# Latent attention of one transformer block: scores of four heads side by side, value products in pairs, output projection k by k

## The chip, the cores and the metric

The kernel runs on one core of a Trainium2 chip. The metric is the device time of one execution in microseconds (us). Five engines work beside each other, each through its own instructions in a fixed order: PE (TensorE, matmuls), DVE (VectorE), ACT (ScalarE), POOL (GpSimd) and SP, whose queue issues the loads of the weights. An instruction that waits for another engine holds back all that stand behind it on its own engine.

## The reference, cut to what matters

256 tokens of width 1024 go through a mixer, a feed-forward layer, latent attention, a second feed-forward layer, and then a second block with attention and a gated feed-forward layer. The change touches latent attention alone:

```
cq, ckv, kr = split(h @ w_in, [384, 640])
q  = (rms_norm(cq, q_g) @ w_uq).reshape(b, s, 16, 64 + 32)
kv = (rms_norm(ckv, kv_g) @ w_ukv).reshape(b, s, 16, 64 + 64)
q_rope, k_rope = apply_rope(q[..., 64:]), apply_rope(kr)
qf = concat([q[..., :64], q_rope]);  kf = concat([kv[..., :64], k_rope for every head])
pr = softmax(qf @ kf * 96 ** -0.5)
x  = x + (pr @ kv[..., 64:]) @ w_out
```

So each of the 16 heads has 64 plain and 32 rotated rows for its scores; the rotated key is the same for all heads.

## The kernel before

All activations are kept with features on the 128 partitions and the 256 tokens along the row. A weight comes as a chunk of up to 1 MB from HBM (`raw`), and is split on the core into a high part (`whi`, ACT, L149) and the rest (`wlo`, DVE or POOL, L152). Each product is then three matmuls in a one-pass type (`three`, L367 to L370: high by high, high by low, low by high). Three `raw` buffers and four pairs of split buffers go round; the SP queue issues the next load when the split before it is done (`Stream`, L125).

The program is built by a scheduler that sets the order on each engine from its own timeline. `Later` (L79) holds pieces of work until so many "ticks" of matmul time have been emitted.

Latent attention stands between the two feed-forward layers:

- `tgemm(XH, XL, KB, 5, c_evac, ...)` (L975): the input projection, five tiles of 128 features (two for keys and values, three for queries). `c_evac` (L944) scales each tile by its gain, splits it into `ch` and `cl`, squares it and lets POOL add the squares. For the two key tiles the split waits until the statistic is known (`kv_split`, L938).
- `rkv_chain` and `rq_chain`: a column sum by PE (L917), a few small operations on DVE, a power on POOL (L925), and for the keys a broadcast over partitions by PE (L342) from `dg`, which DVE makes (L335, L336).
- `thin` (L363) and `fold` (L980) give the rotated key of 32 rows, which a DMA copies to 16 heads (L989).
- `uq_evac` and `uk_evac` put the queries and keys head by head into `qT` and `kT`, 96 rows each.
- Then the heads, one at a time (`attend`, L1068): `sc` makes the scores by two matmuls of 96 rows in full fp32 (L1028; the trace has two records for each), DVE takes the maximum (L1032, L1033), ACT the exponential (L1035), DVE divides by the sum (L1041, L1043), `tr` transposes four blocks (L1050), DVE or ACT copies them (L1052), `pv` multiplies with the values (L1062), and for every second head ACT and DVE split the result (L1065, L1066). Stages of different heads are staggered.
- The output projection is a `tgemm` over eight tiles (L1095 ff.), with the last heads between its first matmuls, and `residual` (L490) adds each result to `x`.

The second block's attention (L1214 to L1290) already works on two heads at once: `sc(j)` sets 64 rows of one head beside 64 rows of the other (L1219) and `pv(j)` sets the 64 value columns of the two heads beside each other (L1269). PSUM holds eight tiles of 128x512: four of the tag `mm`, four of the tag `aux`.

Of the kernel before, what the change touches and what calls it, by code (L numbers as in the profile page):

```python
# [30 lines left out]
PAD_W = 4800 // 4  # L31
# [162 lines left out]
def block_kernel(ctx, tc, a, out):  # L194
# [40 lines left out]
    fold = gap.tile([P, 32], F32, name="fold")  # L235
    cosT = gap.tile([P, T], F32, name="cosT")
# [5 lines left out]
    for n in ("w_va", "w_qk01", "w_qk23", "w_vb", "w_u", "w_oa", "w_ab_out", "w1_0", "w2_0", "w_cin",  # L242
              "w_uq", "w_uk", "w_uv", "w_c_out", "w1_1", "w2_1", "w_qk2", "w_v2",
              "w_o2", "w_gu4", "w_gu", "w_down"):
# [37 lines left out]
    for i in range(2, 4):  # L282
        pool.tensor_tensor(fold, fold, ident[:, 32 * i:32 * i + 32], op=ALU.add)

# [610 lines left out]
    with tc.tile_pool(name="mla", bufs=1) as ap:  # L895
        mpc = tc.tile_pool(name="mlt", bufs=2)
        mp = mpc.__enter__()
        ckv = mp.tile([P, 2, T], F32, tag="ckv", name="ckv", bufs=1)
        ch = ap.tile([P, 5, T], F32R, name="ch")
        cl = ap.tile([P, 5, T], F32R, name="cl")  # L900
        qT = ap.tile([96, NH, T], F32, name="qT")
        kT = ap.tile([96, NH, T], F32, name="kT")
        v = ap.tile([P, 2, D], F32, name="v")
        yh = ap.tile([P, KB, T], F32R, name="yh")
        yl = ap.tile([P, KB, T], F32R, name="yl")
# [32 lines left out]
        def kv_split():  # L938
            for j in range(2):
                dve.tensor_tensor(ckv[:, j], ckv[:, j], rbc[1], op=ALU.mult)  # L940
                act.activation(ch[:, j], ckv[:, j], AF.Copy)
                dve.tensor_tensor(cl[:, j], ckv[:, j], ch[:, j].bitcast(F32), op=ALU.subtract)

        def c_evac(m, ps):  # L944
            for i in range(ps.shape[1]):
# [4 lines left out]
                if kv:  # L950
                    act.activation(ckv[:, j], ps[:, i], AF.Copy, scale=g)
                else:
                    act.activation(ch[:, j], ps[:, i], AF.Copy, scale=g)
                    dve.scalar_tensor_tensor(cl[:, j], ps[:, i], g, ch[:, j].bitcast(F32), op0=ALU.mult,
                                             op1=ALU.subtract)
# [8 lines left out]
                if j == 1:  # L964
                    later(2.0, rkv_chain)
                if j == 4:
                    later(3.5, rq_chain)
# [7 lines left out]
        tgemm(XH, XL, KB, 5, c_evac, lead=4, psums={4: auxt})  # L975

        kr4 = tmp.tile([P, T], F32, tag="rs", name="kr4")
        act.activation(kr4, thin(wkr, "c_norm"), AF.Copy)
        pk = auxt()
        pe.matmul(pk[0:32, 0:T], fold, kr4, start=True, stop=True)  # L980
        SHUF = [(i + 16) % 32 for i in range(32)]
        kr = mp.tile([32, T], F32, tag="kr", name="kr", bufs=1)
        dve.tensor_tensor(kr, pk[0:32, 0:T], rbc[0][0:32], op=ALU.mult)
        k2 = mp.tile([32, T], F32, tag="k2", name="k2", bufs=1)
        dve.stream_shuffle(k2, kr, SHUF)
        pool.tensor_tensor(kr, kr, cosT[0:32], op=ALU.mult)
        dve.tensor_tensor(k2, k2, sinT[0:32], op=ALU.mult)
        dve.tensor_tensor(kr, kr, k2, op=ALU.add)
        nc.sync.dma_start(kT[64:96], spread(kr.unsqueeze(1), 1, NH))  # L989

        def uq_evac(m, ps):

            if m < 4:
                for i in range(2):
                    qs = mp.tile([P, T], F32, tag="qs", name="qs")
                    q2 = mp.tile([P, T], F32, tag="q2", name="q2")
                    act.activation(qs, ps[:, i], AF.Copy)
                    dve.stream_shuffle(q2, qs, SHUF)
                    pool.tensor_tensor(qs, qs, cosT, op=ALU.mult)
                    dve.tensor_tensor(q2, q2, sinT, op=ALU.mult)  # L1000
                    for j in range(4):
                        rr = slice(32 * j, 32 * j + 32)
                        (dve if j < 2 else pool).tensor_tensor(qT[64:96, 4 * (m + i) + j], qs[rr], q2[rr], op=ALU.add)
            else:
                h = 2 * (m - 4)
                q4 = qT[0:64, h:h + 4].rearrange("p (a b) t -> p a b t", b=2)
                act.activation(q4[:, :, 0], ps[0:64], AF.Copy)
                act.activation(q4[:, :, 1], ps[64:128], AF.Copy)

        tgemm(per_k(ch, 5)[2:5], per_k(cl, 5)[2:5], 3, 12, uq_evac, bpc=12)  # L1010

        def uk_evac(m, ps):
            h = 2 * m
            k4 = kT[0:64, h:h + 4].rearrange("p (a b) t -> p a b t", b=2)
            act.activation(k4[:, :, 0], ps[0:64], AF.Copy)
            dve.tensor_copy(k4[:, :, 1], ps[64:128])

        tgemm(per_k(ch, 5)[0:2], per_k(cl, 5)[0:2], 2, 8, uk_evac)
# [4 lines left out]
        st_p, st_t = {}, {}  # L1023

        def sc(h):
            ps = mmt().rearrange("p (a b) -> p a b", a=2)
            for qt in range(2):
                pe.matmul(ps[:, qt], qT[:, h, qt * P:(qt + 1) * P], kT[:, h], start=True, stop=True)  # L1028
            mx = mp.tile([P, 2], F32, tag="mx", name="mx", bufs=3)
            sm = mp.tile([P, 2], F32, tag="sm", name="sm", bufs=4)  # L1030
            pr = mp.tile([P, 2, T], F32, tag="pr", name="pr", bufs=4)
            dve.tensor_reduce(mx, ps, axis=AX, op=ALU.max)  # L1032
            dve.tensor_tensor(mx, mx, nsrq, op=ALU.mult)  # L1033
            for qt in range(2):
                S.behind = act.activation(pr[:, qt], ps[:, qt], AF.Exp, scale=srq[:, qt:qt + 1],  # L1035
                                          bias=mx[:, qt:qt + 1], accum_out=sm[:, qt:qt + 1])
            st_p[h] = (pr, sm)

        def nrm(h):
            pr, sm = st_p[h]  # L1040
            dve.reciprocal(sm, sm)  # L1041
            for qt in range(2):
                dve.tensor_scalar(pr[:, qt], pr[:, qt], sm[:, qt:qt + 1], None, op0=ALU.mult)  # L1043

        def tr(h):
            pr, sm = st_p.pop(h)
            ps = auxt().rearrange("p (a b) -> p a b", a=2)
            for kt in range(2):
                for qt in range(2):
                    pe.transpose(ps[:, kt, qt * P:(qt + 1) * P], pr[:, qt, kt * P:(kt + 1) * P], ident)  # L1050
            pT = mp.tile([P, 2, T], F32, tag="pT", name="pT", bufs=2)
            (act.activation(pT, ps, AF.Copy) if h % 2 else dve.tensor_copy(pT, ps))  # L1052
            st_t[h] = pT

        def pv(h):
            pT = st_t.pop(h)
            if h % 2 == 0:
                state["o"] = auxt()
            o = state["o"]
            rr = slice(64 * (h % 2), 64 * (h % 2) + 64)  # L1060
            for kt in range(2):
                pe.matmul(o[rr, 0:T], v[:, kt, h * 64:(h + 1) * 64], pT[:, kt], start=kt == 0, stop=kt == 1)  # L1062
            if h % 2:
                j = h // 2
                act.activation(yh[:, j], o[:, 0:T], AF.Copy)  # L1065
                dve.tensor_tensor(yl[:, j], o[:, 0:T], yh[:, j].bitcast(F32), op=ALU.subtract)  # L1066

        def attend(i):  # L1068

            if 0 <= i - 3 < NH:  # L1070
                tr(i - 3)
            if 0 <= i - 4 < NH:
                pv(i - 4)
            if 0 <= i - 1 < NH:
                nrm(i - 1)
            if i < NH:
                sc(i)

        wh, wl = S.get()
        for n in range(2):  # L1080
            for tt in range(2):
                ts = slice(tt * P, (tt + 1) * P)
                ps = auxt()
                for k in range(2):
                    s = slice(k * D + n * 512, k * D + n * 512 + 512)
                    pe.matmul(ps, ch[:, k, ts], wh[:, s], start=k == 0, stop=False)
                    pe.matmul(ps, ch[:, k, ts], wl[:, s], start=False, stop=False)
                    pe.matmul(ps, cl[:, k, ts], wh[:, s], start=False, stop=k == 1)
                act.activation(v[:, tt, n * 512:(n + 1) * 512], ps, AF.Copy)
                if n + tt:  # L1090
                    attend(n + n * tt + (1 - n) * (tt - 1))
        S.done()
        for i in range(3, NH):
            attend(i)
# [425 lines left out]
```

## Time and profile before

| | us |
|---|---|
| three runs, median (lowest to highest) | 915.9 (913.51 to 918.45) |
| the profiled execution, its own time | 918.1 |
| span from first to last instruction in it | 916.4 |
| PE busy in the span | 889.9 (97%) |
| DVE, ACT, POOL busy | 583.3, 481.3, 268.0 |
| mean granted clock of TensorE, share of full | 0.988 |

Busy time of PE counts matmuls that overlap in the pipeline, so the distance from one start to the next is what a matmul costs. In a row of the timeline, the first number is the start in us from the span's start, the second how long the row's instructions lasted together, "x4" how many records it merges; at the end stands, in brackets, how long the engine was idle before and on what it waited.

### The profile page before, as it was taken

How to read it: one execution, taken by the hardware profiler on the slowest of the kernel's cores; microseconds unless marked ns; L12 is line 12 of the kernel's file. 1: busy time of each engine (PE TensorE's matmuls, PEld its weight loads, DVE VectorE, ACT ScalarE, POOL GpSimd, SP SyncE). 2: the span in 40 equal slices, each digit the busy share in tenths (PEclk: the TensorE clock that was granted, in tenths of full speed). 3: DMA queues.
4: the chain of work that ended last, by engine and by line, in shares of the span. 5: the costliest groups of instructions: out<-in, count | busy, mean ns of one | idle time of the engine just before them, and what ended most of it. 6: DMA issues, size and time to landing. Idle time of an engine off the chain costs nothing.

```text
span 916.4 us, 16411 instructions
## 1 busy us (share of the span) xinstructions
PE 889.9 (97%) x6680; PEld 824.1 (90%) x6680; DVE 583.3 (64%) x943; ACT 481.3 (53%) x848; POOL 268.0 (29%) x269
## 2 busy tenths in 40 slices
PE   7899999999999998999999999999999999999997
PEld 5788999999999987679999999999967789999885
DVE  7697889555555379846755555547783766666442
ACT  6675467555444275756555544424376665544331
POOL 5876733333011266047333301110147000000000
PEclk9999999999999998999999999999999999999999
DMA  8543454655554336014565555549432465555521
GB/s 293 199 150 126 142 187 161 230 189 191 188 191 164 109 116 230 1 57 150 207 211 189 191 187 191 185 164 248 189 138 93 174 246 191 194 185 189 189 82 46
DMA packets 26107, 154.90 MB, mean 169 GB/s; under 512 B 2752, under 2 KB 5744, under 8 KB 8752
## 3 DMA queue, kind: packets, MB, share of 16 engines
q1 hardware_dynamic: 22704, 148.70, 45.6%
q10 hardware_dynamic: 3040, 4.36, 1.9%
q8 instruction: 52, 0.85, 0.4%
q0 software_dynamic: 288, 0.79, 0.3%
q14 instruction: 23, 0.19, 0.1%
HBM read 152.25 MB, written 1.07 MB: 167 GB/s over the span
## 4 chain that ended last, share of the span: by engine, by line
PE 58%; DVE 1%; issue 0%; ACT 0%; DVEq 0%; POOLq 0%; ACTq 0%
PE mm L368 12%; PE mm L369 12%; PE mm L370 12%; PE aux L466 2%; PE aux L465 2%; PE aux L467 2%; PE mm L1028 2%; PE aux L1062 2%; PE mm L430 2%; PE mm L432 2%; PE mm L431 2%; PE aux L1050 1%; PE mm L465 1%; PE mm L467 1%; PE mm L466 1%; PE aux L1219 1%
## 5 line engine op out<-in xcount | busy, mean ns | idle before, releaser
L149 ACT ACTIVATE whi<-raw 128x1024 fp32r<-128x1024 f32 (+3 forms) x318 | 284.9, 949 | 240.2 <-PE mm L369 157.0
L152 DVE TENSOR_TENSOR wlo<-raw,whi 128x1024 fp32r<-128x1024 f32 (+2 forms) x254 | 307.5, 1246 | 124.4 <-ACT whi L149 122.7
L368 PE MATMUL mm<-xh,whi 128*128 128x256 f32 x1072 | 301.4, 281 | 0.8 <-DVE head L494 0.8
L369 PE MATMUL mm<-xl,whi 128*128 128x256 f32 x1072 | 299.1, 279 | 0.0
L370 PE MATMUL mm<-xh,wlo 128*128 128x256 f32 x1072 | 299.0, 279 | 0.0
L370 PEld LDWEIGHTS mm<-xh,wlo 128*128 128x128 f32 x1072 | 203.9, 190 | 0.0
L368 PEld LDWEIGHTS mm<-xh,whi 128*128 128x128 f32 x1072 | 202.0, 188 | 1.7 <-DVE head L494 1.0
L369 PEld LDWEIGHTS mm<-xl,whi 128*128 128x128 f32 x1072 | 202.0, 188 | 0.2
L368 PE MATMUL mm<-hh,whi 128*128 128x256 f32 x512 | 143.9, 281 | 0.0
L369 PE MATMUL mm<-hl,whi 128*128 128x256 f32 x512 | 143.9, 281 | 0.0
L370 PE MATMUL mm<-hh,wlo 128*128 128x256 f32 x512 | 143.9, 281 | 0.0
L152 POOL TENSOR_TENSOR wlo<-raw,whi 128x512 fp32r<-128x512 f32 (+2 forms) x64 | 84.5, 1349 | 67.0 <-ACT whi L149 66.9
L370 PEld LDWEIGHTS mm<-hh,wlo 128*128 128x128 f32 x512 | 98.3, 192 | 0.0
L368 PEld LDWEIGHTS mm<-hh,whi 128*128 128x128 f32 x512 | 96.1, 188 | 0.0
L369 PEld LDWEIGHTS mm<-hl,whi 128*128 128x128 f32 x512 | 96.1, 188 | 0.0
L519 POOL TENSOR_TENSOR fu<-ft 128x512 f32<-128x512 f32 (+1 forms) x36 | 54.7, 1521 | 119.3 <-ACT ft L517 111.6
L313 POOL TENSOR_TENSOR s_acc<-s_acc,sq 128x256 f32<-128x256 f32 x37 | 43.9, 1193 | 155.2 <-ACT sq L312 144.6
L1120 POOL TENSOR_TENSOR r<-v,nhalf 128x1 f32<-128x1 f32 x4 | 2.2, 557 | 193.5 <-DVE v L1119 193.5
L430 PE MATMUL mm<-whi,xh 128*128 128x512 f32 x96 | 39.1, 424 | 1.9 <-ACT whi L149 1.9
L431 PE MATMUL mm<-wlo,xh 128*128 128x512 f32 x96 | 38.1, 400 | 2.2 <-DVE wlo L152 2.2
L520 DVE TENSOR_TENSOR hl<-fu,hh 128x512 fp32r<-128x512 f32 (+1 forms) x36 | 24.1, 675 | 23.4 <-POOL fu L519 23.4
L432 PE MATMUL mm<-whi,xl 128*128 128x512 f32 x96 | 37.9, 398 | 0.6 <-DVE xl L1329 0.6
(370 smaller groups left out, 1355.7 us busy)
## 6 DMA issues: line engine op xcount, KB each, us to landing
raw<-in_w_dram SPq DMA_DIRECT2D x64, 1024.0 KB, 4.8
raw<-in_w_gu_dram SPq DMA_DIRECT2D x22, 1024.0 KB, 4.8
raw<-in_w_qk_dram SPq DMA_DIRECT2D x12, 1024.0 KB, 6.1
raw<-in_w_down_dram SPq DMA_DIRECT2D x11, 1024.0 KB, 4.8
raw<-in_w_ab_out_dram SPq DMA_DIRECT2D x4, 1024.0 KB, 4.9
raw<-in_w_c_out_dram SPq DMA_DIRECT2D x4, 1024.0 KB, 4.8
raw<-in_w_v_dram SPq DMA_DIRECT2D x4, 1024.0 KB, 6.1
raw<-in_w_o_dram SPq DMA_DIRECT2D x4, 1024.0 KB, 4.9
```

Source lines behind the costliest of these rows:

```text
L149: self.nc.scalar.activation(hi[:, s], r[:, s], AF.Copy)
L152: eng.tensor_tensor(lo[:, s], r[:, s], hi[:, s].bitcast(F32), op=ALU.subtract)
L313: state["sum"] = (dve if k == last else pool).tensor_tensor(acc, acc, sq, op=ALU.add)
L368: pe.matmul(ps, wh, h, start=start, stop=False)
L369: pe.matmul(ps, wh, l, start=False, stop=False)
L370: pe.matmul(ps, wl, h, start=False, stop=stop)
L430: pe.matmul(pss[tt], h[k][:, ts], wh[:, s], start=k == 0, stop=False)
L431: pe.matmul(pss[tt], h[k][:, ts], wl[:, s], start=False, stop=False)
L432: pe.matmul(pss[tt], l[k][:, ts], wh[:, s], start=False, stop=k == nk - 1)
L465: pe.matmul(ps, h[k][:, ts], wh[:, ns], start=k == 0, stop=False)
L466: pe.matmul(ps, h[k][:, ts], wl[:, ns], start=False, stop=False)
L519: pool.tensor_tensor(u[:, 0:g], t[:, 0:g], t[:, 0:g], op=ALU.mult)
```

## The change

Latent attention is written anew; nothing else changes but two small tables and the layout of three weights.

- The key tiles are split at once, as the query tiles are; the statistic is applied later, to the keys when they are copied from PSUM (`k_nope`) and to the values (`values`). The key chain starts after more ticks (3.7 for 2.0), and its broadcast stands 4.0 ticks behind for 2.0.
- The rotated key is made on all 128 partitions (`fold4`), so the DMA to 16 heads falls away. Queries and keys of two heads lie on one tile (64 rows each), rotated queries of four heads on one tile (32 rows each).
- `sc(a)` handles four heads: eight matmuls of 64 rows, in pairs, then eight of 32 rows, in fours, added into the same four `aux` tiles. `nrm`, `tr` and `pv` go by pairs of heads; POOL divides one head of a pair.
- PE's order is written out by hand: between the scores of one group of four and the next stand the projections of the next group and a piece of the values. Then the output projection goes k by k over all eight tiles (four `mm` tiles), with `pv` and `tr` of the next pairs between.

```diff
         def rkv_chain():
             lat_rms(rkv, "kv", 256)
-            bcast(rbc[1], rkv, dt=2.0)
-            later(2.1, kv_split)
+            bcast(rbc[1], rkv, dt=4.0)
...
-                    later(2.0, rkv_chain)
+                    later(3.7, rkv_chain)
...
+        mctx = tc.manual_schedule(engines={mybir.EngineType.PE})
+        mctx.__enter__()
...
+        def sc(a):
+            pss = [auxt().rearrange("p (a b) -> p a b", a=2) for _ in range(4)]
+            for p in range(2):
+                for qt in range(2):
+                    for i, rr in enumerate(HALF):
+                        pe.matmul(pss[2 * p + i][:, qt], qn[a][rr, p, qt * P:(qt + 1) * P], kn[a][rr, p],
+                                  start=qt == 0, stop=False)
+            for qt in range(2):
+                for i in range(4):
+                    rr = slice(32 * i, 32 * i + 32)
+                    pe.matmul(pss[i][:, qt], qr[rr, a, qt * P:(qt + 1) * P], kr[rr], start=False, stop=qt == 1)
+            later.tick(2.6)
+            for p in range(2):
...
+                for i in range(2):
+                    dve.tensor_reduce(mx[:, i], pss[2 * p + i], axis=AX, op=ALU.max)
+                dve.tensor_tensor(mx, mx, spread(nsrq.unsqueeze(1), 1, 2), op=ALU.mult)
+                for i in range(2):
+                    for qt in range(2):
+                        S.behind = act.activation(prs[i][:, qt], pss[2 * p + i][:, qt], AF.Exp,
...
+        sc(0)
+        q_nope(w, 1)
+        S.done(held=3)
+        k_nope(wk, 1)
+        values(wv, 0, 1)
+        nrm(0)
+        nrm(1)
+        sc(1)
...
+        sc(3)
+        tr(0)
+        values(wv, 1, 1)
+        S.done()
+        nrm(6)
+        nrm(7)
+        pv(0)
+        tr(1)
...
+        for k in range(6):
+            if k % 2 == 0:
+                w = S.get()
+            for n in range(2):
+                if n:
+                    (tr(k + 2) if k + 2 < 8 else None)
+                else:
+                    pv(k + 1)
+                for m in range(4 * n, 4 * n + 4):
+                    c_out(w, m, k)
```

What this does to the order of instructions is seen at three places. First PE, at the scores. Before, the scores of five heads stand at the front, then one head after another (L1028 scores, L1050 transposes, L1062 value products):

```order
L1088 MATMUL aux<-whi,cl 128x512
L1028 MATMUL mm<-kT,qT 128x256 x10
L1050 MATMUL aux<-ident,pr 128x128
L1028 MATMUL mm<-kT,qT 128x256 x2
L1050 MATMUL aux<-ident,pr 128x128 x3
L1028 MATMUL mm<-kT,qT 128x256 x2
```

and now, from the values ahead of the second group to the query projection behind it:

```order
L1026 MATMUL mm<-whi,ch 128x512
L1027 MATMUL mm<-wlo,ch 128x512
L1028 MATMUL mm<-whi,cl 128x512
L1057 MATMUL aux<-kn,qn 128x256 x8
L1062 MATMUL aux<-kr,qr 128x256 x8
L371 MATMUL mm<-ch,whi 128x256
```

The scores of four heads stand together, with no transposes near them, and projections follow at once.

Second ACT, at the exponentials. Before (L1035 exponentials, L1052 copies of transposes, L1065 splits of results):

```order
L1035 ACTIVATE pr,sm<-mm,mx,srq 128x256 x4
L1065 ACTIVATE yh<-aux 128x256
L1052 ACTIVATE pT<-aux 128x512
L1035 ACTIVATE pr,sm<-mm,mx,srq 128x256 x4
L1065 ACTIVATE yh<-aux 128x256
```

and now (L1073 exponentials, L1013 the copy of the next group's queries, L1030 values), for groups 0 to 2:

```order
L1073 ACTIVATE pr,sm<-aux,mx,srq 128x256 x8
L1013 ACTIVATE qn<-mm 128x512
L149 ACTIVATE whi<-raw 128x768 x2
L1030 ACTIVATE v<-mm,rkv 128x512
L1073 ACTIVATE pr,sm<-aux,mx,srq 128x256 x8
L1013 ACTIVATE qn<-mm 128x512
L1030 ACTIVATE v<-mm,rkv 128x512
```

The exponentials of a group stand in one run of eight, and the copy that the next scores need stands behind them.

Third DVE, between the statistic of the keys and the broadcast matrix `dg`. Before (L923, L924, L926 the chain, L335 and L336 `dg`):

```order
L923 TENSOR_TENSOR lr<-aux,r_3638 128x2
L954 SCALAR_TENSOR_TENSOR cl<-mm,head,ch 128x256
L954 SCALAR_TENSOR_TENSOR cl<-aux,head,ch 128x256
L924 TENSOR_SCALAR lr<-lr 128x2
L926 TENSOR_TENSOR rkv<-lr,r_col_84 128x2
L335 TENSOR_SCALAR dg<-ident,rkv 128x128 x2
L336 SCALAR_TENSOR_TENSOR dg<-ident,rkv,dg 128x128 x2
```

and now (L928, L929, L931 the chain, L338 and L339 `dg`):

```order
L929 TENSOR_SCALAR lr<-lr 128x2
L982 TENSOR_TENSOR kr<-aux,rbc_86 128x256
L1007 STREAM_SHUFFLE q_3910<-qr 128x256 x2
L931 TENSOR_TENSOR rkv<-lr,r_col_84 128x2
L983 STREAM_SHUFFLE k_3922<-kr 128x256
L1009 TENSOR_TENSOR q_3910<-q_3910,sinT 128x256 x2
L338 TENSOR_SCALAR dg<-ident,rkv 128x128 x2
L985 TENSOR_TENSOR k_3922<-k_3922,sinT 128x256
L1010 TENSOR_TENSOR qr<-qr,q_3910 128x256
L339 SCALAR_TENSOR_TENSOR dg<-ident,rkv,dg 128x128
L1010 TENSOR_TENSOR qr<-qr,q_3910 128x256
L1007 STREAM_SHUFFLE q_3950<-qr 128x256
```

The rotation of key and queries has moved between the steps of the chain; the second half of `dg` follows right behind the last row.

## Rows read from the trace of the kernel before

**Rows 1.** Timeline of PE: first matmul of the query projection, first matmul of the next feed-forward layer.
```profile
327.48 0.50 PE L368 MATMUL mm<-ch,whi 128*128 128x256 f32 x2
...
428.23 0.28 PE L368 MATMUL mm<-xh,whi 128*128 128x256 f32 x1
```
**Rows 2.** Timeline of PE: the two longest waits of the stage.
```profile
344.85 0.86 PE L1087 MATMUL aux<-wlo,ch 128*128 128x512 f32 x2 [2.62 <-POOL wlo L152]
...
362.35 7.95 PE L1028 MATMUL mm<-kT,qT 96*128 96x256 f32 x20 [2.83 <-DVE kT L1016]
```
**Rows 3.** Timeline of PE: one head, and the start of the next.
```profile
380.12 1.03 PE L1028 MATMUL mm<-kT,qT 96*128 96x256 f32 x4
381.08 1.08 PE L1062 MATMUL aux<-pT,v 128*64 128x256 f32 x4
382.09 0.66 PE L1050 MATMUL aux<-ident,pr 128*128 128x128 f32 x4
382.58 1.03 PE L1028 MATMUL mm<-kT,qT 96*128 96x256 f32 x4
```
**Rows 4.** Timeline of PE, second block's attention: scores and value product of two heads.
```profile
657.48 0.93 PE L1219 MATMUL aux<-kT,qT 64*128 64x128 f32 x8
...
675.85 0.87 PE L1269 MATMUL aux<-pT,v 128*64 128x256 f32 x8
```
**Rows 5.** Timeline of PE: `thin` in four column tiles, first key-projection matmul, first matmul after 48.
```profile
328.53 1.07 PE L363 MATMUL aux<-head,ws 128*32 128x256 f32 x16
...
351.83 0.28 PE L368 MATMUL mm<-ch,whi 128*128 128x256 f32 x1
...
357.30 0.39 PE L1087 MATMUL aux<-wlo,ch 128*128 128x512 f32 x1
```
**Rows 6.** Timeline of PE: the statistic of the keys, and its broadcast.
```profile
327.99 0.61 PE L917 MATMUL aux<-ones,sqa 128*128 128x1 f32 x4
...
334.52 0.28 PE L342 MATMUL aux<-dg,ones_r 128*128 128x256 f32 x1
```
**Rows 7.** Timeline of POOL: weight splits, sum of squares, power.
```profile
325.27 1.98 POOL L152 TENSOR_TENSOR wlo<-raw,whi 128x384 fp32r<-128x384 f32 x2 [6.61 <-ACT whi L149]
327.21 0.72 POOL L962 TENSOR_TENSOR sqa<-sq 128x256 f32<-128x256 f32 x1
327.90 2.69 POOL L152 TENSOR_TENSOR wlo<-raw,whi 128x384 fp32r<-128x384 f32 x2
330.73 0.71 POOL L925 TENSOR_TENSOR lr<-lr,nhalf 128x2 f32<-128x2 f32 x1
```
**Rows 8.** Timeline of ACT: weight split, and exponentials with a copy between them.
```profile
353.00 2.01 ACT L149 ACTIVATE whi<-raw 128x1024 fp32r<-128x1024 f32 x2 [2.08 <-DMA raw<-in_w_c_out_dram]
...
373.02 0.56 ACT L1035 ACTIVATE pr<-mm,mx,srq 128x256 f32<-128x256 f32 x1
...
373.56 0.59 ACT L1052 ACTIVATE pT<-aux 128x512 f32<-128x512 f32 x1
374.04 0.57 ACT L1035 ACTIVATE pr<-mm,mx,srq 128x256 f32<-128x256 f32 x1
```
**Rows 9.** Timeline of DVE: rotation, weight split, division, maximum, scaling.
```profile
336.52 0.44 DVE L998 STREAM_SHUFFLE q<-qs 128x256 f32<-128x256 f32 x1
...
359.21 2.36 DVE L152 TENSOR_TENSOR wlo<-raw,whi 128x1024 fp32r<-128x1024 f32 x2
...
371.01 0.61 DVE L1043 TENSOR_SCALAR pr<-pr,sm 128x256 f32<-128x256 f32 x2
...
371.61 0.67 DVE L1032 TENSOR_REDUCE mx<-mm 128x2 f32<-128x512 f32 x1
372.20 0.15 DVE L1033 TENSOR_TENSOR mx<-mx,nsrq 128x2 f32<-128x2 f32 x1
```
**Rows 10.** Stretches: busy us of PE, PEld, DVE, ACT, POOL, then granted clock, DMA.
```profile
345.00:347.00 2.00, 2.00 (x10) 1.85 (x10) 2.00 (x2) 0.23 (x1) 2.00 (x2) 0.57 0.87 365
...
364.00:366.00 2.00, 2.00 (x6) 1.55 (x6) 0.97 (x3) 0.35 (x1) 0.00 (x0) 0.50 0.80 336
```

More of the change, by code (lines that the diff above doesn't have):

```diff
@@ L30 @@
 PAD_X = 1216 // 4
[L31 removed]
+PAD_W = 4800 // 4 - P
 WARM_UP = 8
@@ L975, in block_kernel @@
         tgemm(XH, XL, KB, 5, c_evac, lead=4, psums={4: auxt})
+        SHUF = [(i + 16) % 32 for i in range(32)]
         kr4 = tmp.tile([P, T], F32, tag="rs", name="kr4")
+        mctx = tc.manual_schedule(engines={mybir.EngineType.PE})
+        mctx.__enter__()
         act.activation(kr4, thin(wkr, "c_norm"), AF.Copy)
[L979 to L1008, printed above, removed]
@@ new lines, in q_nope, with k_nope, values @@
+        def q_nope(w, g):
+            S.behind = act.activation(qn[g], tiles(w, 6 * (g % 2), CK[2:5], CL[2:5], 3, 2), AF.Copy)
+        def k_nope(w, g):
+            ps = tiles(w, 4 * g, CK[0:2], CL[0:2], 2, 2)
+            for i in range(2):
+                dve.tensor_tensor(kn[g][:, i], ps[:, i], rbc[1], op=ALU.mult)
+        def values(w, n, tt):
+            ts = slice(tt * P, (tt + 1) * P)
+            ps = mmt()
+            wh, wl = w
+            for k in range(2):
+                s = slice(k * D + n * 512, k * D + n * 512 + 512)
+                pe.matmul(ps, ch[:, k, ts], wh[:, s], start=k == 0, stop=False)
+                pe.matmul(ps, ch[:, k, ts], wl[:, s], start=False, stop=False)
+                pe.matmul(ps, cl[:, k, ts], wh[:, s], start=False, stop=k == 1)
+            later.tick(1.3)
+            act.activation(v[:, tt, n * 512:(n + 1) * 512], ps, AF.Copy, scale=rkv[:, tt:tt + 1])
@@ L1055, in pv @@
[L1055 to L1091, printed above, removed]
@@ new lines, in pv @@
+        def pv(j):
+            pTs = st_t.pop(j)
+            o = auxt()
+            for kt in range(2):
+                for i, rr in enumerate(HALF):
+                    pe.matmul(o[rr, 0:T], v[:, kt, (2 * j + i) * 64:(2 * j + i + 1) * 64], pTs[i][:, kt],
+                              start=kt == 0, stop=kt == 1)
+            later.tick(0.9)
+            if j % 2 == 0:
+                state["yh"] = ap.tile([P, 2, T], F32R, tag="q", name="yh", bufs=4)
+                state["yl"] = ap.tile([P, 2, T], F32R, tag="k", name="yl", bufs=4)
+            yh[j], yl[j] = state["yh"][:, j % 2], state["yl"][:, j % 2]
+            S.behind = act.activation(yh[j], o[:, 0:T], AF.Copy)
+            dve.tensor_tensor(yl[j], o[:, 0:T], yh[j].bitcast(F32), op=ALU.subtract)
@@ L1097, in block_kernel @@
+        w = S.get()
+        for g in range(4):
+            if g == 0:
+                pv(7)
+            for m in (2 * g, 2 * g + 1):
+                for k in (6, 7):
+                    c_out(w, m, k)
+            residual(2 * g, pss[g], s_acc[1], "ffn_norm1")
+        S.done()
+        mctx.__exit__(None, None, None)
         mpc.__exit__(None, None, None)
```

158 lines of the change are left out of this document (102 added, 56 removed).

## The prediction

> **What bounds the kernel now.** I read the busy table first (PE 97%), then PE's timeline from the projection of the queries to the next feed-forward layer, since all that the change touches stands between these two rows: 327.5 to 428.2, a stage of 100.7 us [rows 1]. Then I set against it what PE has to do there, by the distance from start to start. 48 projection matmuls of 256 columns take 5.47 us, 0.114 each [rows 5]; a matmul of 512 columns counts as two. One head costs 0.96 for scores, 1.01 for the value product and 0.49 for transposes, 2.46 together [rows 3]. So the work is 16 x 2.46 = 39.4 for the heads, 348 x 0.115 = 40.0 for projections (156 inwards, 192 outwards), 24 x 0.23 = 5.5 for the values, and some 2.7 for the rotated key, statistics and broadcast (1.0 of it the four-column-tile product [rows 5]): 87.6 us. The other 13.1 us are waits and a slow clock. Two waits, of 2.62 and 2.83 us, stand out [rows 2], and in the stretches behind them TensorE was granted 0.57 and 0.50 of its full clock [rows 10], the lower of its two levels, 1.2 of 2.4 GHz. Outside this stage nothing moves, so I ask one thing: how long the new stage is.
>
> **Work that goes.** *Scores.* A matmul of 96 rows and 256 columns costs 0.96 / 2 = 0.48, and 16 heads 15.4. In the second block two heads of 64 rows lie side by side: four matmuls, which one by one would be 0.24 + 0.24 + 0.48 + 0.48 = 1.44, last 0.93 [rows 4]. So a pair costs what a single one does, and changing the tiling some 0.1 to 0.2. A group of four heads now has four such pairs, 1.92, and two fours of 32 rows. No row shows four row tiles. From below, four column tiles do run at once: eight matmuls of 256 columns in 1.07 [rows 5], so two fours cost 0.96; from above, one after another, 8 x 0.48 = 3.84. I take 0.96, since rows 5 and rows 4 both show tiles overlapping fully. A group is 1.92 + 0.96 + 0.2 = 3.1, four groups 12.4: 3.0 less.
>
> The Trainium skill, "TensorE: Matmul & The Clock Gate", part 3, gives four tiles of 32 rows a speedup of 3.07, not 4; as an estimate from that page the fours would be 3.84 / 3.07 = 1.25, and the whole forecast 1.2 us later.
>
> *Value products.* The second block's pair has three quarters of the columns and lasts 0.87 [rows 4]; with all columns I take 1.05. Eight pairs make 8.4 where 16 heads made 16.2: 7.8 less. Transposes and projections keep their number; the outward one, k by k, has the same 192 matmuls. The DMA of the rotated key goes, and stands in no chain that ends here. PE's work is 87.6 - 10.8 = 76.8 us.
>
> **Waits that come.** PE's order is now fixed, so each late operand stops all behind it. I walk the new order with durations of the rows.
>
> *Statistic of the keys.* PE comes to it 1.5 us into the stage. POOL adds the squares behind four weight splits, which before took 1.98 + 2.69 with the sum between them [rows 7]; now all four stand ahead. From the same start of 325 they end at 329.6, and with 0.72 for the sum it is 330.3: a wait of 1.6 (between 0.5 and 2.5).
>
> *Broadcast of the keys' scale.* From statistic to broadcast 6.5 us passed before [rows 6]. Now the power on POOL stands behind a split of 512 columns (1.3 to 1.9, as the 384-column splits scale [rows 7]) and another sum of 0.72, and on DVE nine operations of the rotation at 0.44 [rows 9] stand between the steps. That makes 8.5 us, and PE has 5.0 us of work for it: a wait of 3.2 (1.0 to 5.0; the lower end is near the 6.5 of before). The third quarter of the value weights, behind ACT and POOL, adds 0.7 (0 to 1.5). The matmuls that run inside these waits are small ones, already counted.
>
> *Between groups.* All four `aux` tiles belong to one group, and the copy of the next queries stands on ACT behind eight exponentials. From the end of the scores: two maxima at 0.6 and a scaling of 0.1 [rows 9], eight exponentials at 0.54 from start to start [rows 8], a copy of 0.5 [rows 8], hand-overs 0.2: 6.4 us. In two of the groups all four maxima and both scalings come ahead of the first exponential: 1.2 more. Before the second scores the next keys are scaled on DVE behind two divisions, 0.6 more. PE's work in between is 30 x 0.114 + 6 x 0.23 = 4.8 us, and only 3.4 ahead of the last scores. Waits: 7.0 - 4.8 = 2.2, 7.7 - 4.8 = 2.9, 7.7 - 3.4 = 4.3 us, together 9.4 (7.0 to 11).
>
> The Trainium skill, "TensorEngine Tiling (Array Packing)", PSUM Bottleneck, warns that tiling speeds up TensorE but not the emptying of PSUM. By that rule a group lasts as long as its emptying, 3.1 + 6.4 to 7.7, as in my sum; by PE's rows alone it would last 3.1 + 4.8, and the stage would be 9.4 us shorter.
>
> *Behind the last scores.* Three splits of 1.18 [rows 9] stand on DVE ahead of its maxima (1.5 late), then maxima, scaling and the first two exponentials (2.5), before the first transpose finds a free `aux` tile: 4.0. The second waits 0.6 for two exponentials more. The copy of its transposes stands on ACT behind eight exponentials, a split of 1.0 [rows 8] and one of half that: PE waits 2.4 for it and 0.5 for the next. Together 7.5 (5 to 9). In the output projection copies have 1.4 us of matmuls ahead of them and are hidden, until the last pair, whose split on ACT and DVE costs 0.8; a late first feed-forward operand may add 0.5: 1.3.
>
> The waits make 1.6 + 3.2 + 0.7 + 9.4 + 7.5 + 1.3 = 23.7, and the stage 76.8 + 23.7 = 100.5 us: 0.2 less than now. Ten microseconds of work would be paid back in waits.
>
> **The clock.** Behind each of the two waits of before the clock was at half for 3.5 us (345 to 348.5) and 7 us (362.3 to 369.4) [rows 2, 10]. The new stage has six waits between 2.2 and 4.3 us. Where a group's scores run at half clock, 3.1 us become 4.8 (a slow stretch of 3.5) to 6.2 (of 7), and what hangs on them moves with them: I take 2.2 for each of three groups. The broadcast loses 0.9 more (its slow matmuls partly lie beside the wait for value weights), the value products behind the last scores 1.5. Against that, 1.5 comes back, since slow last scores cover DVE's three splits. Sum 7.5 (0 to 11).
>
> **The sum.** -0.2 + 7.5 = +7.3 us against the profiled execution's own 918.1: 925.4. The median of the runs stands 2.2 below that execution, so 923 us.
>
> **The rivals.**
> *The clock stays full.* The place is the wait ahead of the scores of groups 1 to 3; it decides whether these waits reach about 2.6 us, the shortest single wait that a slow clock followed [rows 2, 10]. Mine are 2.2, 2.9 and 4.3. If they stay just below that, the stage is 100.5 and the time 918.1 - 0.2 - 2.2 = 916: not slower. For it: the exponentials could start 0.6 earlier if DVE's maxima do not bunch. Against it: the last wait has little work to hide it.
>
> *The chains are short.* The change takes the copies of queries and keys in halves, and the additions for single heads, off ACT, DVE and POOL ahead of the heads. If the engines then slow each other less, the early waits fall to their lower ends (5.5 to 1.5), the end to 5.0, and no wait is long enough for the clock: 916 - 4.0 - 2.5 = 909, faster. Against it: what stands in the way is mainly order on the engines.
>
> *The fours do not overlap.* Then each group's scores take 2.9 more, all of it on the chain: 923 + 11.6 = 935.
>
> **How the numbers follow.** My forecast has 0.48 (its own range 918 to 930), the full clock 0.23, short chains 0.25, fours one by one 0.04. Measurement tells 0.5%, 4.6 us, from no change: below 911.3 is faster, above 920.5 slower. Faster is the short chains, 0.25. Same is the full clock and the low edge of the forecast, 0.23 + 0.04. The rest is 0.48. The range leaves out the top case and the lower part of the short chains, and takes in most of the bounds: 906 to 930.
>
> **What would show it.** Right: one pair of half-matmuls lasts about 0.48; eight exponentials behind one another between scores; waits on ACT ahead of the second, third and fourth scores; a wait on DVE at the broadcast; a granted clock near 0.5 in scores. Wrong: the fourth group's scores done before 372, PE busy without gaps between groups, or a full clock throughout.

## The result, and the profile after

The changed kernel takes 925.2 us (median of 4 runs, 924.1 to 928.6), the kernel before beside it 915.0 (913.5 to 918.5): a ratio of 1.0112, with a 95% interval of 1.0072 to 1.0152. It is slower by some 10 us; the forecast was 923, in a range of 906 to 930.

PE's timeline of the stage comes first. Of the changed kernel it has these rows (shared lines of the program stand 3 lines lower: L368 is now L371). In them `sqa` are the added squares, `kn` and `qn` the scaled keys and the copied queries that the scores read, `pr` the exponentials, `pT` their transposes.

```profile
328.00 1.07 PE L366 MATMUL aux<-head,ws 128*32 128x256 f32 x16
330.17 0.38 PE L371 MATMUL mm<-ch,whi 128*128 128x256 f32 x1 [1.10 <-ACT sq L951]
...
332.47 1.02 PE L922 MATMUL aux<-ones,sqa 128*128 128x1 f32 x4 [1.69 <-POOL sqa L957]
...
341.79 0.36 PE L345 MATMUL aux<-dg,ones_r 128*128 128x256 f32 x1 [0.86 <-DVE dg L338]
343.56 0.38 PE L345 MATMUL aux<-dg,ones_r 128*128 128x256 f32 x1 [1.42 <-DVE dg L339]
...
350.63 0.51 PE L1027 MATMUL mm<-wlo,ch 128*128 128x512 f32 x1 [0.94 <-POOL wlo L152]
...
351.29 2.00 PE L1057 MATMUL aux<-kn,qn 64*128 64x256 f32 x16
353.22 1.15 PE L1062 MATMUL aux<-kr,qr 32*128 32x256 f32 x16
354.30 0.38 PE L371 MATMUL mm<-ch,whi 128*128 128x256 f32 x1
...
362.06 3.45 PE L1057 MATMUL aux<-kn,qn 64*128 64x256 f32 x16 [2.72 <-DVE kn L1018]
...
374.47 2.00 PE L1057 MATMUL aux<-kn,qn 64*128 64x256 f32 x16 [2.58 <-ACT qn L1013]
...
385.24 2.75 PE L1057 MATMUL aux<-kn,qn 64*128 64x256 f32 x16 [3.96 <-ACT qn L1013]
...
392.81 0.82 PE L1093 MATMUL aux<-ident,pr 128*128 128x128 f32 x4 [2.86 <-ACT pr L1073]
...
437.17 0.39 PE L371 MATMUL mm<-xh,whi 128*128 128x256 f32 x2
438.95 0.39 PE L372 MATMUL mm<-xl,whi 128*128 128x256 f32 x1 [1.39 <-DVE xl L303]
```

The next feed-forward layer begins at 437.2 where it began at 428.2 [rows 1]. The scores are short: a group takes 3.0 us (351.29 to 354.30). But where the stage before had two waits above 1 us [rows 2], this one has seven, and several shorter ones. From 402 us on, in the output projection, there are none.

In the stretches (busy us of PE, PEld, DVE, ACT, POOL, then granted clock, DMA) the clock is low behind most waits, but not behind all:

```profile
332.00:338.00 6.00, 5.53 (x24) 5.36 (x25) 1.46 (x5) 1.77 (x4) 3.74 (x5) 0.50 0.79 296
...
362.00:366.00 4.00, 3.94 (x24) 3.18 (x28) 2.02 (x3) 1.03 (x2) 0.79 (x1) 0.57 0.20 45
...
374.00:378.00 4.00, 3.53 (x36) 2.71 (x37) 1.42 (x4) 1.00 (x2) 2.02 (x3) 1.00 0.02 4
386.00:389.00 3.00, 3.00 (x24) 2.02 (x24) 2.84 (x3) 2.02 (x3) 0.99 (x2) 0.56 0.00 0
393.00:396.00 3.00, 2.68 (x11) 2.12 (x11) 1.41 (x4) 3.00 (x13) 1.85 (x2) 0.53 0.00 0
```

For the account I cut the stage alike in every kernel, from the last matmul of the input projection to the first of the next feed-forward layer, and add up PE's timeline: waits above 0.2 us, the loss by the clock (half of the time in which PE worked at half clock), and the rest, which is work at full clock.

| kernel | ratio to before (95% interval) | stage | waits | clock | work |
|---|---|---|---|---|---|
| before | 1 | 101.1 | 6.4 | 5.1 | 89.7 |
| changed | 1.0112 (1.0072 to 1.0152) | 109.4 | 19.2 | 9.7 | 80.4 |
| e1 queries a group ahead | 1.0091 (1.0069 to 1.0112) | 106.1 | 16.1 | 8.6 | 81.4 |
| e2 query weights off POOL | 1.0162 (1.0135 to 1.019) | 114.9 | 22.1 | 13.1 | 79.7 |
| e3 waits filled | 1.0088 (1.0062 to 1.0114) | 106.7 | 11.0 | 5.1 | 90.6 (9.7 of it filling) |
| e4 first transposes in mm | 1.0144 (1.0122 to 1.0166) | 110.3 | 20.3 | 9.5 | 80.5 |
| e5 = e1 + order on DVE | 1.0041 (1.0027 to 1.0055) | 102.5 | 11.8 | 8.6 | 82.2 |
| e6 = e5 + tail rearranged | 0.9972 (0.9956 to 0.9989) | 96.4 | 11.0 | 3.2 | 82.3 |
| e7 = e6 + early chain | 0.9927 (0.99 to 0.9954) | 93.2 | 8.0 | 3.4 | 81.8 |
| e9 = e7 + key chain first | 0.9896 (0.9856 to 0.9935) | 88.9 | 5.6 | 1.7 | 81.6 |
| e8 output by tiles | 1.0125 (1.0103 to 1.0146) | 109.5 | 20.3 | 9.2 | 80.0 |

So the change takes 9.2 us of work off PE, and adds 12.9 of waits and 4.6 of clock: 8.2 us more in the stage. In the next layer, 1.39 and 0.63 us of waits on DVE stand where 0.84 was. Ahead of the stage nothing was changed, and there profiles of one code differ by some us: the input projection ends between 323.5 and 327.8 in the profiles of these kernels. So stages are compared here, not spans. A stage too comes from one profiled execution; that of the changed kernel took 3.4 us more than its median, that of e2 3.8 more, that of e4 2.5 less. Up to the first scores the changed kernel, e3, e4 and e8 have the same code, and take 23.5, 22.6, 22.3 and 23.5 us there, so a difference of 1 us between two rows says nothing.

### The profile page after: what moved, and what is told of

The parts are those of the page before. It is cut to its first block, busy times and chain, and to the rows that moved or that the text cites. A ratio compares the mean times of both kernels' runs of the same rounds, so it can differ in the third digit from the quotient of the medians.

```text
span 926.9 us, 16497 instructions
## 1 busy us (share of the span) xinstructions
PE 885.7 (96%) x6744; PEld 822.5 (89%) x6744; DVE 567.6 (61%) x909; ACT 475.1 (51%) x836; POOL 272.8 (29%) x281
## 4 chain that ended last, share of the span: by engine, by line
PE 56%; ACT 3%; DVE 2%; issue 1%; POOL 0%; DVEq 0%; POOLq 0%; ACTq 0%
PE mm L371 12%; PE mm L372 12%; PE mm L373 12%; PE aux L469 2%; PE aux L468 2%; PE aux L470 2%; ACT pr L1073 2%; PE mm L433 2%; PE mm L435 2%; PE mm L434 1%; PE aux L1057 1%; PE aux L1105 1%; PE mm L468 1%; PE mm L470 1%; DVE mx L1069 1%; PE mm L469 1%
## 5 line engine op out<-in xcount | busy, mean ns | idle before, releaser
L152 DVE TENSOR_TENSOR wlo<-raw,whi 128x1024 fp32r<-128x1024 f32 (+2 forms) x254 | 302.7, 1228 | 126.4 <-ACT whi L149 124.7
L371 PE MATMUL mm<-xh,whi 128*128 128x256 f32 x1072 | 299.2, 282 | 0.0
L371 PEld LDWEIGHTS mm<-xh,whi 128*128 128x128 f32 x1072 | 201.3, 189 | 0.6 <-issue 0.4
L371 PE MATMUL mm<-hh,whi 128*128 128x256 f32 x512 | 143.9, 281 | 0.0
L371 PEld LDWEIGHTS mm<-hh,whi 128*128 128x128 f32 x512 | 96.1, 188 | 0.0
```

Of the source, the lines that this page charges most:

```text
L152: eng.tensor_tensor(lo[:, s], r[:, s], hi[:, s].bitcast(F32), op=ALU.subtract)
L371: pe.matmul(ps, wh, h, start=start, stop=False)
```

## The experiments

My theory after this: the work went as forecast, and is paid back because PE, its order fixed, stands behind late operands; each of the waits is order on ACT, DVE and POOL, and the clock adds to it. Rivals: the clock alone; the drain of the four `aux` tiles, whatever the order; the new output projection.

**Is the clock an effect of the waits, and what does it cost?** Matmuls that nobody reads were set where PE waits.

```diff
+        def fill(n, w):
+            ps = mmt()
+            for _ in range(n):
+                pe.matmul(ps, ch[:, 0, 0:P], w[0][:, 0:512], start=True, stop=True)
...
+        fill(9, wv)
         sc(1)
...
+        fill(9, wv)
         sc(2)
...
+        fill(14, wv)
         sc(3)
+        fill(10, wv)
         tr(0)
```

> Matmuls whose results nobody reads (9, 9, 14 and 10 of 512 columns, 0.23 us each at full clock) stand where PE waits 2.72, 2.58, 3.96 and 2.86 us: ahead of the second, third and fourth scores and of the first transposes. The output stays the reference's. Theory (these waits themselves bring the half clock that follows; a busy PE keeps it full): the granted clock is 1.00 from 350 us to the end of the stage, the slow stretches at 362, 386 and 393 us are gone, and the stage is 2 to 4 us shorter though no wait ends sooner. Rival (the clock falls for another reason, or what it costs is hidden behind the chain on DVE and ACT): no change, or up to 1 us more by the added matmuls.

The stage is 2.7 us shorter with 9.7 us more matmuls in it. Of this 0.9 lies ahead of the first filling, where the code is the same; from the first scores to the end it is 84.1 us for 85.9. (The medians, 923.2 and 925.2, lie too close for their intervals to part them.) In e3's stretches the second and the fourth scores run at full clock:

```profile
361.00:366.00 5.00, 4.90 (x48) 4.24 (x49) 3.83 (x7) 1.29 (x3) 0.83 (x1) 1.00 0.32 103
...
383.00:388.00 5.00, 5.00 (x41) 3.98 (x42) 5.00 (x7) 1.76 (x2) 0.72 (x1) 1.00 0.23 72
...
391.00:395.00 4.00, 4.00 (x12) 2.42 (x12) 3.39 (x8) 4.00 (x12) 3.61 (x4) 0.57 0.01 4
```

So with the waits filled the scores kept the full clock, and that is worth some 2 us, just short of the 2 to 4 of the theory. A slow stretch at 391 us stayed, behind waits of only 1.27 and 0.48. The larger part, the waits, is not the clock's doing.

**What do the second to fourth scores wait for?** First the queries' copy was taken from behind the exponentials.

```diff
         values(wv, 0, 0)
+        q_nope(w, 1)
+        S.done(held=3)
...
         sc(0)
-        q_nope(w, 1)
-        S.done(held=3)
+        w = S.get()
+        q_nope(w, 2)
...
         sc(1)
-        w = S.get()
-        q_nope(w, 2)
+        q_nope(w, 3)
...
         sc(2)
-        q_nope(w, 3)
```

> The projection of a group's plain queries stands one group earlier on PE, so that its copy on ACT stands ahead of the eight exponentials and not behind them; nothing else moves. Theory (order behind the scores sets the waits: exponentials, then the copy, on ACT): the wait of the second scores on the copy is gone; the scores start when the keys are scaled, about 6.8 us behind the end of the last scores where it is 7.8 now. 3 x 1.0 us less, and the 2.0 us of the projection of the second group no longer fill a wait, so 1 to 2 us less without the clock, and 3 to 4 less if the slow stretch in the second and fourth scores goes: ratio to before about 1.008. Rival (the four aux tiles alone set the waits, the copy lies beside them): the scores start no earlier than now and the stage gets 2 us longer. The wait before the fourth scores gets longer under both, since only 1.4 us of projections are left there.

PE's timeline of e1, second to fourth scores and first transposes:

```profile
360.94 2.00 PE L1059 MATMUL aux<-kn,qn 64*128 64x256 f32 x16 [1.64 <-DVE kn L1018]
...
370.54 2.00 PE L1059 MATMUL aux<-kn,qn 64*128 64x256 f32 x16 [1.53 <-DVE kn L1018]
...
377.53 0.70 PE L1059 MATMUL aux<-kn,qn 64*128 64x256 f32 x2 [2.34 <-ACT pr L1075]
...
388.19 2.23 PE L1095 MATMUL aux<-ident,pr 128*128 128x128 f32 x8 [3.29 <-ACT pr L1075]
```

and a stretch of e1 (busy us, granted clock, DMA):

```profile
379.00:393.00 14.00, 10.69 (x45) 6.67 (x42) 10.94 (x22) 10.66 (x30) 8.83 (x8) 0.51 0.21 75
```

Scores follow each other at 9.7 and 9.6 us, where 10.8 and 12.4 stood; the keys, scaled on DVE behind a division, are next in line. The second scores start 6.7 us behind the end of the first, as the theory said, so the four tiles alone did not set that wait. The stage gains 3.3 us, some 0.9 of it ahead of the first scores, and the whole times (medians 923.9 and 925.2) do not part the two kernels. Little of the gain comes from the clock: 379 to 393 us are now one slow stretch (0.51), behind waits of 2.34 and 3.29.

Then DVE's order was set by hand (`issue_after` lets the instructions in its block be issued only behind the one that it names):

```diff
+                with tc.issue_after(state["mx"].ins) if p else nullcontext():
                     for i in range(2):
                         dve.tensor_reduce(mx[:, i], pss[2 * p + i], axis=AX, op=ALU.max)
...
+            with tc.issue_after(state["kn"].ins):
                 dve.reciprocal(sm, sm)
```

> On top of the queries a group ahead (e1), the order on DVE: the keys of the next group are scaled ahead of both divisions, and the maxima of the second pair of heads stand behind the scaling of the first pair's. In e1 the second and third scores waited 1.6 us each for the scaled keys. Theory (what stands between them on DVE is what the scores wait for): the scores then wait for the first four exponentials alone, whose end is about 4 us behind the scores while PE has 4.8 us of projections: both waits fall below 0.6, the distance from scores to scores from 9.6 to about 8.2, and the stage from 106.1 to 103 to 104. Rival (the aux tiles of the second pair of heads are free only behind all eight exponentials and stop the scores in their middle): a new wait of 1 us or more inside the scores, and the stage gets less than 1 us shorter. The fourth scores still wait over 2 us under both: only 1.4 us of projections stand ahead of them.

```profile
348.25 2.00 PE L1059 MATMUL aux<-kn,qn 64*128 64x256 f32 x16
356.25 2.50 PE L1059 MATMUL aux<-kn,qn 64*128 64x256 f32 x16
364.75 2.34 PE L1059 MATMUL aux<-kn,qn 64*128 64x256 f32 x16
371.35 5.02 PE L1059 MATMUL aux<-kn,qn 64*128 64x256 f32 x16 [1.57 <-DVE kn L1018]
```

The waits ahead of the second and third scores are gone; these come 8.0 and 8.5 us behind the ones before. Their first part takes 2.5 and 2.34 us for 2.0, so a wait inside them, which the rival looked for, is at most 0.5. The theory's numbers held (the stage, 102.5, is a little below its 103 to 104). So at that place the emptying of four tiles is not the bound by itself: with the right order it fits beside 4.8 us of projections.

**What sets the end?** A free tile alone does not do it:

```diff
-        def tr(j):
+        def tr(j, psum=auxt):
...
         sc(3)
-        tr(0)
+        tr(0, mmt)
```

> The transposes of the first pair go to two tiles of the tag mm, which are idle there, in place of two aux tiles that the fourth scores hold. Theory (PE waits 2.86 us behind the fourth scores for a free aux tile alone; the operands are there since 362): that wait is gone, the transposes and the values follow the scores at once; the value product behind them then waits for a free aux tile instead, until 392, with about 2.4 us of work done by then: 1.5 to 2.5 us less. Rival (the later chain, copies on ACT behind the exponentials, sets the end): the wait moves to the value product and the stage gets less than 0.5 us shorter.

```profile
385.45 1.09 PE L1093 MATMUL mm<-ident,pr 128*128 128x128 f32 x8
...
389.18 0.62 PE L1105 MATMUL aux<-pT,v 128*64 128x256 f32 x2 [1.24 <-DVE pT L1095]
393.62 1.97 PE L1105 MATMUL aux<-pT,v 128*64 128x256 f32 x6 [3.82 <-ACT pT L1095]
```

The rival is right. The transposes run at once, and the value product waits 1.2 and then 3.8 us for their copies, the second of which ACT makes behind eight exponentials. There is no gain: from the first scores on the stage is 2.2 us longer than the changed kernel's (88.0 for 85.9). So the tail was put into another order as a whole, on top of e5, and the first chunk of output weights is split on POOL and not on DVE:

```diff
-           "w_cin": (2,), "w_uq": (1,), "w_uv": (0,), "w_c_out": (2, 3),
+           "w_cin": (2,), "w_uq": (1,), "w_uv": (0,), "w_c_out": (0, 2, 3),
...
         k_nope(wk, 3)
+        tr(0, mmt)
+        values(wv, 1, 1)
...
+        pv(0, mmt)
         sc(3)
-        tr(0)
-        values(wv, 1, 1)
+        tr(1, mmt)
...
         for k in range(6):
...
+            for m in range(4):
+                c_out(w, m, k)
+            pv(k + 1)
...
+            for m in range(4, 8):
+                c_out(w, m, k)
+            if k < 5:
+                tr(k + 2)
```

> On top of e5, the work behind the third scores: the transposes, the values' last quarter and the value product of the first pair stand ahead of the fourth scores, in tiles of the tag mm; the second pair's transposes follow in mm tiles, and the output projection's first step comes before the next value product. The first chunk of output weights is split earlier, on POOL, so that DVE's three splits no longer stand ahead of the last maxima. Theory (the waits behind the third and fourth scores, 2.7 and 3.8 us in e1, and the half clock from 379 to 393, come from PE having nothing that is ready): both waits fall below 1 us together, the clock is full from 355 us on, and the stage is 7 to 10 us shorter than e1's 106.1: 96 to 99, ratio to before 0.995 to 1.0. Rival (copies on ACT behind the exponentials, which these steps need too, set the end): the wait moves to the first output matmuls or the next value product, and the stage stays above 101.

```profile
373.39 1.03 PE L1097 MATMUL mm<-ident,pr 128*128 128x128 f32 x8
...
376.04 1.42 PE L1109 MATMUL mm<-pT,v 128*64 128x256 f32 x8 [0.22 <-DVE pT L1099]
377.39 2.31 PE L1059 MATMUL aux<-kn,qn 64*128 64x256 f32 x16
380.70 1.09 PE L1097 MATMUL mm<-ident,pr 128*128 128x128 f32 x8
...
384.22 0.62 PE L1109 MATMUL aux<-pT,v 128*64 128x256 f32 x2 [1.03 <-DVE mx L1073]
```

```profile
350.00:390.00 40.00, 36.42 (x292) 28.77 (x290) 28.04 (x62) 28.79 (x84) 21.10 (x20) 1.00 0.22 80
```

The fourth scores start without a wait, and from 350 to 390 us the clock is full (1.00, PE busy 36.4 of 40.0 us). The stage is 9.7 us below e1's, 6.1 below e5's, and of these 6.1 the clock gives 5.4 (8.6 to 3.2 in the table); how much the order on PE and how much the split on POOL did was not parted. The kernel is now faster than the one before. The theory's 96 to 99 held, though waits of 2.4 us in all remain behind the fourth scores, more than the 1 us it allowed.

**The start.** Taking POOL's splits of query weights away (`ON_POOL` without `w_uq`) from the changed kernel:

> The split of the second chunk of query weights goes from POOL to DVE, so POOL adds the squares of the key tiles as soon as they are there. Theory (POOL's four splits make PE late at the statistic of the keys; that wait and the one before it bring the half clock from 331.7 to 338.6, and the late statistic makes the broadcast late): the wait of 1.69 us at the statistic and the 2.3 us at the broadcast are gone or below 0.5 each, the clock is full there, and the start of the first scores comes 4 to 6 us earlier; DVE has 1.8 us more, which costs up to 1. Rival (the broadcast waits on DVE's rotation, not on the statistic): the wait at the broadcast grows by what the statistic gives back, and the first scores come less than 2 us earlier.

```profile
338.14 0.40 PE L345 MATMUL aux<-dg,ones_r 128*128 128x256 f32 x2
...
347.52 0.79 PE L1027 MATMUL mm<-wlo,ch 128*128 128x512 f32 x1 [4.85 <-POOL wlo L152]
...
362.58 3.48 PE L1057 MATMUL aux<-kn,qn 64*128 64x256 f32 x16 [4.22 <-DVE kn L1018]
```

The waits at the broadcast are gone, as the theory said, but this run does not show why: the scheduler also put the keys' scale and the first steps of `dg` ahead of the rotation on DVE. The theory is half right on the statistic, which still waits 1.19; the rival is right on the gain: the first scores start 21.6 us behind the input projection for 23.5, only 1.9 sooner. What was won at the broadcast is spent at the values, which wait 4.85 for a split on POOL behind the rotation. The second scores then wait 4.2 for their keys, since DVE's order has changed too: a split of the next query weights now stands ahead of them. The clock took 3.4 us more. In e7 and e9 the start was mended on top of e6, whose order behind it is fixed (`high_priority` and `hot` make the scheduler set these steps ahead of others):

```diff
-           "w_cin": (2,), "w_uq": (1,), "w_uv": (0,), "w_c_out": (0, 2, 3),
+           "w_cin": (2,), "w_c_out": (0, 2, 3),
...
-                act.activation(sq, ps[:, i], AF.Square)
+                with tc.high_priority(offset=AHEAD) if kv else nullcontext():
+                    act.activation(sq, ps[:, i], AF.Square)
...
-                    later(3.7, rkv_chain)
+                    later(3.7, lambda: hot(rkv_chain))
...
         w = S.get()
+        S.force(3 + S.n_use - 1)
```

(The last line emits all weight splits up to the values' at this point.)

> On top of e6, the start: no split of query or value weights on POOL, the squares of the key tiles ahead of the weight splits on ACT, the key chain ahead of what stands beside it, and the value weights split on DVE while it waits for the chain. Theory (the waits at the first projection, the statistic, the broadcast and the value weights, 1.1 + 1.7 + 2.6 + 1.0 us in e1, and two slow stretches behind them, come from order on POOL, ACT and DVE): together they fall to 1.5 or less, and the first scores come 5 to 7 us sooner: ratio about 0.99. Rival (the key chain is long by itself: statistic, power on POOL, scale, four steps of the diagonal, broadcast): the broadcast still waits 1.5 us or more and brings the slow clock, and the gain is below 3 us; DVE's 4.2 us of splits may also delay the first keys.

```profile
336.37 0.36 PE L345 MATMUL aux<-dg,ones_r 128*128 128x256 f32 x1 [0.78 <-DVE dg L338]
338.25 0.39 PE L345 MATMUL aux<-dg,ones_r 128*128 128x256 f32 x1 [1.52 <-DVE dg L339]
```

e7's first scores start 22.5 us behind the input projection (25.5 in e6), and the wait for the value weights is gone. But as the rival said the broadcast still waits 2.3 us, and 3.0 us sooner is less than the 5 to 7 of the theory. In e9, on DVE, rotation and value weights go behind the diagonal, the steps of `dg` (each with `issue_after` the last step of `dg`), and all of `c_evac` has the high priority:

> On top of e7, which still waited 0.8 + 1.5 us at the broadcast and had a slow stretch behind it: on DVE the two steps of the statistic, the scale and the four steps of the diagonal come one behind another, the rotation and the split of the value weights behind them. Theory (the broadcast waited for rotation and splits that stood between the steps on DVE, and for the squares of the queries on POOL ahead of the power): the diagonal is ready before PE comes to it, both waits are gone, the slow stretch at 340 us too, and the kernel is 2 to 4 us faster than e7: ratio to before about 0.989. Rival (the rotation, now later, is what the first scores wait for): the wait moves to the 32-row products of the first scores or to the first keys, and the gain is below 1 us.

```profile
335.47 0.40 PE L346 MATMUL aux<-dg,ones_r 128*128 128x256 f32 x2
...
342.53 2.00 PE L1068 MATMUL aux<-kn,qn 64*128 64x256 f32 x16
```

What stood in the way is seen between the power of the keys' statistic on POOL (`lr`) and the keys' scale on DVE (`rkv`). In the changed kernel:

```profile
334.79 0.71 POOL L930 TENSOR_TENSOR lr<-lr,nhalf 128x2 f32<-128x2 f32 x1
...
337.78 0.43 DVE L982 TENSOR_TENSOR kr<-aux,rbc 128x256 f32<-128x256 f32 x1 [3.61 <-PE aux L980]
...
338.82 0.58 DVE L931 TENSOR_TENSOR rkv<-lr,r_col 128x2 f32<-128x2 f32 x1
```

The power was done at 335.5, but the scaling of the rotated key (`kr`) stood ahead of `rkv` on DVE and waited for PE's own product (L980), which stands behind projections there. In e9 `rkv` comes first:

```profile
330.22 0.68 DVE L932 TENSOR_TENSOR rkv<-lr,r_col 128x2 f32<-128x2 f32 x1 [0.82 <-POOL lr L931]
```

So the chain was not long by itself, as the rival of e7 had it: its order made it long. In e9's stretches the clock from 333 on is nearly full:

```profile
333.00:345.00 12.00, 12.00 (x101) 11.24 (x103) 10.88 (x30) 4.70 (x8) 5.29 (x8) 0.99 0.26 92
```

PE is busy without a gap from 333 to 345, nothing waits for the rotation, and the kernel takes 905.6 us (904.2 to 907.5) against 915.0 of the kernel before: faster than both, 9.4 us below the kernel before and some 20 below the changed one.

**The output projection.** One part was undone alone: by tiles, four over all k and then two at a time, with the heads between the first k.

```diff
...
+        tgemm(yh, yl, KB, 8, lambda m, ps: residual(m, ps, s_acc[1], "ffn_norm1"), lead=4,
+              pre={j: lambda j=j: heads(j) for j in range(7)})
```

> One part of the change undone alone: the output projection goes by tiles as before (four tiles over all k, then two at a time), with the pairs' transposes and value products between the k of the first four tiles; weights in the old layout. Theory (k by k needs one chunk of weights at its start, by tiles needs two, and the second is loaded and split late): PE waits 3 to 5 us for the second chunk ahead of the first output matmuls and the clock falls again: 3 to 7 us slower than the changed kernel, ratio 1.015 to 1.02. Rival (the order of k and tiles is worth nothing by itself, the heads between are hidden either way): within 1 us of the changed kernel.

```profile
401.95 1.09 PE L1093 MATMUL aux<-ident,pr 128*128 128x128 f32 x8
404.35 1.08 PE L1105 MATMUL aux<-pT,v 128*64 128x256 f32 x8
405.37 1.09 PE L1093 MATMUL aux<-ident,pr 128*128 128x128 f32 x8
```

My theory fell here. The second chunk of weights was there in time, no wait stands behind 401 us, and the stage is 109.5 for 109.4 (from the first transposes to its end 43.7 for 44.4; the ratios' intervals overlap). The order of k and tiles by itself makes no difference that these runs can tell.

## Why the prediction was right, point by point

- **Work.** Forecast 10.8 less, measured 9.2. The new parts were sized well: scores 12.0 us for 12.4, value products 8.9 for 8.4, from start to start at full clock. Both totals were too small (87.6 and 76.8 for 89.7 and 80.4), since products of one kind in a row were counted at 0.115 and each change of kind costs some 0.1 more: twelve products between two changes take 1.55 us (404.12 to 405.66) and not 1.38, and the output projection takes 24.5 us, not 22.1, with pairs between its parts.
- **The fours overlap.** Eight products of 32 rows last 1.08 (353.22 to 354.30), near the bound of 0.96 that I took and far from 3.84. The Trainium skill, "TensorE: Matmul & The Clock Gate", part 3, would give 1.25 by its factor of 3.07, as the estimate in the prediction has it; the row is better than that.
- **Start.** Statistic 1.69 for 1.6, broadcast 2.3 for 3.2, value weights 0.9 for 0.7. One wait I had not seen: 1.10 at the first projection, for a tile whose square ACT makes behind two splits of 1024 columns. The first two sizes came out by luck. PE reached the statistic 3.0 us into the stage and not 1.5, and POOL's sum was done at 4.6 and not 3.1. From statistic to broadcast 9.3 us passed and not 8.5, and PE's work in between took 8.5 us and not 5.0, since much of it ran at half clock. (By its own terms the forecast was 8.5 less 5.0, 3.5 and not 3.2.) And I had put the delay on DVE down to nine operations of the rotation, where DVE also stood until 337.8 for PE's product L980, 2.3 us beyond the end of the power.
- **Between groups.** 2.72, 2.58 and 3.96 for 2.2, 2.9 and 4.3, with the releasers as the sum had them (the keys behind divisions at the second scores, the copy behind the exponentials at the third and fourth); the sign that named ACT for the second scores too was at odds with that sum, and did not come. e1 and e5 show the mechanism: with copy and keys out of the way, the waits of the second and third scores went, and the distance fell to 8.0 and 8.5. The Trainium skill, "TensorEngine Tiling (Array Packing)", PSUM Bottleneck, says that tiling does not speed up the emptying of PSUM. That agrees with the changed kernel, whose groups last 10.8 and 12.4 us while their copies are made; e5, at 8.0 and 8.5 where PE's work is some 7.9, shows that most of this was order.
- **End.** Forecast 7.5 (4.0, 0.6, 2.4, 0.5), measured 4.0 (2.86, 0.32, 0.28, 0.51). The slow last scores covered DVE's three splits, as the term of the clock had it. And PE was at half clock from 393.2 to 396.6, so that the values' last quarter (394.7 to 397.1) covered most of the copy that I let PE wait 2.4 for. That the copy stands behind the exponentials and would be the next wait is shown by e4.
- **Clock.** Forecast 7.5, measured 9.7, in part elsewhere. Scores of the second and fourth group ran slow, as said, and the values behind the last; the third group's did not. The longest slow stretch, 331.7 to 338.6, lies behind the first two waits of the stage, where I had put none. In e3, with the waits filled, the scores kept the full clock.
- **The next layer.** 1.2 us more waits there, for the 0.5 that I allowed.

The sum, +7.3 forecast for 10.2 between the medians (8.2 of it in the stage), is nearer than its parts. For the new stage I had 76.8 of work, 23.7 of waits and 7.5 of clock; 80.4, 19.2 and 9.7 were measured. 4.5 too much in waits stands against 3.6 and 2.2 too little in the other two: the mechanism was right, but that the time came out so close is luck. The rivals: the clock did not stay full; the chains were not short as the change has them; the fours did overlap. What short chains promised can be had, though, by other orders than the change has: e9 has the full clock nearly throughout and ends at 905.6, below the 909 that I gave them.

## What to carry to other kernels

Work taken off a busy engine is a gain only if what feeds it in its new order is there in time: walk each late operand back through the engine that makes it, and look at what stands ahead of it there. Where a fixed order on one engine meets scheduled orders on the others, tie the few steps that it waits for (here two orders on DVE, a copy on ACT and the key chain) to their places. Together with another order of PE's tail and other places for a few weight splits, that turned 10 us lost into 9 won, with the same matmuls. Mend such a chain to its end: taking away one wait (e2, e4) only moved it, and in e2 the slow clock took 3.4 us more.

## What the hardware showed that I had not expected

- No length of a single wait foretold the half clock. Behind 2.72 us at 362 it fell (0.57), behind 2.58 at 374 it stayed full (1.00); in e3 it fell behind waits of 1.27 and 0.48 with a few transposes between them (0.57 from 391 to 395), and in e9 behind 0.91 and 1.19 (0.50 from 330 to 333). My "about 2.6 us" was no bound.
- In e1 the clock was low for 14 us in a row (379 to 393, 0.51) though PE was busy for 10.7 of them.
- Filling costs little: with 42 more matmuls of 512 columns (9.7 us) in waits, the stage is 1.8 us shorter from the first scores on.
